# Block-diagonal level products, value products sorted by shape, and one projection moved, in a hybrid encoder layer

## The chip, the cores and the metric

One Trainium2 chip; the kernel runs on one of its cores. The metric is the device time of one execution in microseconds. Before the change three runs took 1318.72, 1318.90 and 1319.15 us; their median is 1318.9.

## The reference

One encoder layer over 1024 tokens of width 1024, in float32. One input projection feeds two groups of heads that run side by side; their outputs are normalised, gated, joined and projected; then come a layer norm, a SwiGLU feed-forward network, a second layer norm and a gated per-layer embedding (PLE). Cut to what the change touches:

```python
# HGRN2, 4 heads of 128, chunkwise:  S_t = diag(f_t) S_{t-1} + k_t (x) v_t,  k_t = 1 - f_t
scores  = einsum('bhtd,bhsd,bhtsd->bhts', q, k, decay)        # decay = exp(b_t - b_s) for s <= t
o       = einsum('bhts,bhsv->bhtv', scores, v) + einsum('bhtd,bhdv->bhtv', q * exp(b), state)
# mLSTM, 4 heads, q and k of 64, v of 128, stabilised, chunkwise
qk  = einsum('bhtd,bhsd->bhts', q, k) * w_intra
num = einsum('bhts,bhsv->bhtv', qk, v) + w_inter * einsum('bhtd,bhdv->bhtv', q, C)
den = sum(qk, -1) + w_inter * einsum('bhtd,bhd->bht', q, n)
# PLE, at the very end
x = x + sigmoid(x @ ple_w_gate + ple_b_gate) * (p @ ple_w_proj)
```

The decay in the HGRN2 scores differs for each of the 128 key channels, so `scores` isn't one matrix product of q and k.

## The kernel before, in words

**Precision.** The large products split each operand into a high and a low part (`split`, lines 75 to 77: a cast on ScalarE, a difference on VectorE) and sum three products in `mm3` (lines 79 to 83), each one record of 128x512 in the trace. The recurrences multiply plain float32, and each such product shows as two records.

**Stages.** `mixers` computes the input projection tile by tile and, between its matmuls, the two recurrences; `out_proj` the output projection and the first layer norm, with the first gate tiles of the network; `ffn_up` and `ffn_down` the network by a seven-product scheme on halves, with PLE at the end. A scheduler places the instructions: it keeps each engine's order near that of the program, but lets a later instruction go first where an earlier one isn't ready. TensorE, VectorE and ScalarE work off their queues in that order; loads are issued on SyncE's queue, stores on ScalarE's.

**The pumps.** Each recurrence is a Python generator with `yield` between its steps. `f_tile` (a tile of 128 projected channels, two halves of 512 tokens, 24 matmuls each) calls `pump` after half of the matmuls and at the end of a half, and `tok_group` and the PLE projection call it too; each call moves every live generator one step on. `finish` runs a generator to a mark or to its end at once. mLSTM's stream runs over all heads, `head(h)` computes f and q of one HGRN2 head and starts its stream, after it has run the head before to its tail. The last eight tiles (`gate_evac`) multiply the mixed values by their gates.

**HGRN2 levels** (`hgrn`, per head and half of the tokens, four chunks of 128). The triangle of scores A is built by levels L = 1, 2, 4, ... 64: at level L each block of 2L positions gets the products of its first half's keys with its second half's queries, and then q and k take in the decay of half a block (lines 567 and 568). For L = 1 (line 537) and L = 2 to 16 (line 556) the kernel multiplies all 128 keys by all 128 queries of a chunk (192 columns in the first product: the diagonal and level 1 together), and keeps the entries that a mask names, by a product with the unit matrix (line 538) and masked copies (lines 539 and 558). For L = 32 and 64 (line 549) it multiplies only the blocks, whose outputs start at partitions 0 and 64, or at 0. Score tiles rotate over three PSUM banks, of which the first product takes two for each half.

**mLSTM values** (`mlstm`, eight chunks). For each of two row halves q and two heads p of it, line 454 multiplies the scores E (128 rows) by the values, and from the second chunk on line 456 adds the state (64 rows) into the same place. The two kinds take turns. Line 465 updates the state with 64 stationary columns.

**PLE projection** (`ple_proj`, in `mixers`). p is multiplied by one half of the projection's columns between heads 1 and 2, by the other between heads 2 and 3; each time both weight tiles of p are loaded and split anew, results go by ScalarE (line 629) to memory, and `pump` is called four times.

**Memory.** Weight tiles of `mixers` and `out_proj` come from the pool wp (two raw, three split tiles). `ffn_up` opens its pools, with the split operands XS2, XS4 and XA22, where wp and out_proj's rows were; a tile there waits until the tile that lay there before is done with.

Of the kernel before, what the change touches and what calls it, by code (L numbers as in the profile page):

```python
# [9 lines left out]
F32 = mybir.dt.float32  # L10
F32R = mybir.dt.float32r
U8 = mybir.dt.uint8
# [6 lines left out]
P = 128  # L19
S = 1024  # L20
D = 1024
# [2 lines left out]
DFF = 2816  # L24
NF = DFF // P
HB = 512
EARLY = 4
NP = NF // 2
KORD = (4, 5, 6, 7, 0, 1, 2, 3)
LEVELS = (1, 2, 4, 8, 16, 32, 64)  # L30
ALPHA = 2.0 ** 0.25
LN_EPS = 1e-5
RMS_EPS = 1e-6
# [98 lines left out]
def mixers(g, es):  # L132
    a, act, dve, pool, pe, sp = g.a, g.act, g.dve, g.pool, g.pe, g.sp
    wtile, mm3, split, mtile = g.wtile, g.mm3, g.split, g.mtile
    kc = es.enter_context(g.tc.tile_pool(reuse_waits="tile", name="kc", bufs=1))
    mx = es.enter_context(g.tc.tile_pool(reuse_waits="tile", name="mx", bufs=2))
    ps = es.enter_context(g.tc.tile_pool(reuse_waits="tile", name="psA", bufs=1, space=PSUM))

    def bank(tag, shape, name):
        return ps.tile(shape, F32, tag=tag, bufs={"ft": 2, "hg": 3, "ml": 3}[tag], name=name)  # L140
# [23 lines left out]
    for k in range(KT):  # L164
        kk, q = divmod(k, 4)
# [6 lines left out]
        for b in range(2):  # L172
            raw = mtile("xraw")
            sp.dma_start(raw, a["xT"][:, k, b * HB:(b + 1) * HB])
            xraw.append(raw)
    for k in range(KT):
        kk, q = divmod(k, 4)
# [4 lines left out]
        for b in range(2):  # L182
            raw = xraw[2 * k + b]
# [22 lines left out]
    def stage(nm):  # L206
        return mx.tile([P, HB], F32, name="st", bufs=2)
# [14 lines left out]
    def pump():  # L222
        for st in list(streams):
            if next(st, "end") == "end":
                streams.remove(st)
# [99 lines left out]
    rcol = [kc.tile([64, P], F32, name=f"rcol{i}") for i in range(2)]  # L325
    for i in range(2):
        dve.memset(rcol[i], 0.0)
    lvl = kc.tile([P, 7, 256], U8)
    for l0, l1 in ((0, 4), (4, 7)):
        n = (l1 - l0) * 256  # L330
        raw = g.wp.tile([P, 1056], F32, name="wraw", bufs=2)
        rv = raw[:, :n].rearrange("p (l t) -> p l t", t=256)
        sp.dma_start(rv, a["lvl"][:, l0:l1])
        dve.tensor_copy(lvl[:, l0:l1], rv)
    ones_row = kc.tile([4, P], F32)
    dve.memset(ones_row, 1.0)
    Cst = kc.tile([P, 2, 129], F32)
    dve.memset(Cst, 0.0)
    mst = [kc.tile([4, 1], F32, name=f"mst{i}") for i in range(2)]
    dve.memset(mst[0], 0.0)  # L340
# [26 lines left out]
    def mlstm(c):  # L367
        i = c % 2
        qk = mx.tile([P, 4, P], F32, name="mqk")
        sp.dma_start(qk, g.mq_d[c])  # L370
        v = mx.tile([P, 4, 129], F32, name="mv")
        sp.dma_start(v[:, :, 0:P], g.mv_d[c].rearrange("p (h d) -> p h d", h=4))
        dve.memset(v[:, :, P:P + 1], 1.0)
        pg = bank("ml", [P, 2, P], "pg")
        pe.transpose(pg[0:4, 0], sm["ig"][:, c], ident)
        pe.transpose(pg[0:4, 1], sm["lf"][:, c], ident)
# [22 lines left out]
        ml = row("ml")  # L399
# [20 lines left out]
        pw = bank("ml", [P, 2, P], "pw")  # L420
        for p in range(2):
            pe.matmul(pw[:, p], sel[:, p], wrow[i], start=True, stop=True)
        qw = mx.tile([P, 2, P], F32, name="qw", bufs=1)
# [4 lines left out]
        pd = bank("ml", [P, 4, P], "pd")  # L428
# [18 lines left out]
        yield  # L447
        views = []
        den = mx.tile([P, 4], F32, name="den")
        for q in range(2):  # L450
            pr = slice(64 * q, 64 * q + 64)
            pn = bank("ml", [P, 2, 129], "pn")
            for p in range(2):
                pe.matmul(pn[:, p], E[:, 2 * p + q], v[:, 2 * p + q], start=True, stop=c == 0)
                if c:
                    pe.matmul(pn[:, p], qw[pr, p], Cst[pr, p], start=False, stop=True)
            dn = den[:, q::2]
            dve.tensor_max(dn, pn[:, :, P], cols[:, 32 + q:36:2])
            dve.scalar_tensor_tensor(dn, pn[:, :, P], -1.0, dn, op0=OP.mult, op1=OP.max)
            views.append((slice(q, 4, 2), pn[:, :, 0:P]))  # L460
        dve.reciprocal(den, den)
        if c < NC - 1:
            pst = bank("ml", [P, 2, 129], "pst")
            for h in range(4):
                pe.matmul(pst[64 * (h % 2):64 * (h % 2) + 64, h // 2], kws[:, h], v[:, h], start=True, stop=True)
            for p in range(2):
                dve.scalar_tensor_tensor(Cst[:, p], Cst[:, p], wold[:, p:p + 1], pst[:, p], op0=OP.mult, op1=OP.add)
# [50 lines left out]
    def hgrn(h, b, q, k, f):  # L518
# [3 lines left out]
        qq = q  # L522
# [5 lines left out]
        def odd(t):  # L528
            return t.rearrange("p c (b two) -> p c b two", two=2)[:, :, :, 1]

        A = mx.tile([P, 4, P], F32, name="A")
        dve.tensor_mul(q1, odd(q), odd(f))
        for c0 in (0, 2):
            cc = slice(c0, c0 + 2)
            pd = bank("hg", [P, 2, 192], "sc")
            for c in range(2):
                pe.matmul(pd[:, c], k[:, c0 + c], qq[:, c0 + c], start=True, stop=True)
            dve.tensor_mul(A[:, cc], pd[:, :, 0:P], ident[:, None, :].to_broadcast([P, 2, P]))
            dve.copy_predicated(odd(A[:, cc]), lvl[:, 0, 0:P].rearrange("p (c b) -> p c b", c=2), pd[:, :, P:192])
        dve.tensor_mul(even(q), even(q), even(f))  # L540
        tot = f.rearrange("p c t -> p (c t)")
        for li, L in enumerate(LEVELS):
            n = 2 * L
            if L >= 32:
                yield
                pd = bank("hg", [P, 4, P], "sc")
                for c in range(4):
                    for s in range(0, P, n):
                        pe.matmul(pd[s:s + L, c, 0:L], k[:, c, s:s + L], q[:, c, s + L:s + n], start=True, stop=True)
                for s in range(0, P, n):  # L550
                    act.copy(A[s:s + L, :, s + L:s + n], pd[s:s + L, :, 0:L])
            elif L > 1:
                yield
                pd = bank("hg", [P, 4, P], "sc")
                for c in range(4):
                    pe.matmul(pd[:, c], k[:, c], q[:, c], start=True, stop=True)
                vw = lambda t: t.rearrange("p h (b n) -> p (h b) n", n=n)[:, :, L:n]
                dve.copy_predicated(vw(A), lvl[:, li].rearrange("p (b l) -> p b l", l=L), vw(pd))
            nb = 256 // L
            tv = tot.rearrange("p (b two) -> p b two", two=2)  # L560
            t4 = tot.rearrange("p (c b two) -> p c b two", c=4, two=2)
            kv = k.rearrange("p h (b n) -> p (h b) n", n=n)[:, :, 0:L]
            if L == 1:
                dve.tensor_mul(odd(q), q1, t4[:, :, :, 0])
            else:
                qv = q.rearrange("p h (b n) -> p h b n", n=n)[:, :, :, L:n]
                dve.tensor_mul(qv, qv, t4[:, :, :, 0:1].to_broadcast([P, 4, nb // 4, L]))
            dve.tensor_mul(kv, kv, tv[:, :, 1:2].to_broadcast([P, nb, L]))
            nt = mx.tile([P, nb], F32, name=f"tot{L}", bufs=1 if L < 64 else 2)
            dve.tensor_mul(nt, tv[:, :, 0], tv[:, :, 1])  # L570
            tot = nt
# [43 lines left out]
        streams.append(head_streams[h])  # L615

    load_btok(520, 512)
    def ple_proj(s):
        pw = wtile(a["wpp"][s])
        for b in range(2):  # L620
            ph, pl = (t[:, :1024].rearrange("p (k t) -> p k t", k=2) for t in wtile(a["pT"][b]))
            for t in range(4):
                tt = slice(t * P, (t + 1) * P)
                pp = bank("ft", [P, 512], "pp")
                for k in range(2):
                    ks = slice(k * HB, (k + 1) * HB)
                    mm3(pp, (ph[:, k, tt], pl[:, k, tt]), tuple(w[:, ks] for w in pw), k == 0, k == 1)
                r = stage("ppo")
                act.copy(r, pp)
                act.dma_start(g.pp_d[4 * b + t, :, s * HB:(s + 1) * HB], r)  # L630
                if t % 2:
                    pump()

    tok_group("wt2", 0, g.hv_d, 0)
    head(0)
    tok_group("wt3", 256, g.hv_d, 256)
    head(1)
    ple_proj(0)
    head(2)
    ple_proj(1)  # L640
    head(3)

    for j in (4, 5, 6, 7, 0, 1, 2, 3):
# [10 lines left out]
def out_proj(g, es):  # L654
# [68 lines left out]
    transposed(1, y1)  # L723
    for f in range(2, EARLY):
        g.early[f] = g.ft.gate0(f)


def x_split(g, t, k0, b, raw=None):
# [385 lines left out]
def _shape_constants():  # L1114
    r = {}
    r["ident"] = np.eye(P, dtype=np.float32)
    s = np.arange(P)
    lvl = np.zeros((P, 7, 4, 64), np.float32)
    for li, L in enumerate(LEVELS):
        tsec = s[(s // L) % 2 == 1]  # L1120
        m = (s[:, None] // (2 * L) == tsec[None] // (2 * L)) & ((s[:, None] // L) % 2 == 0)
        lvl[:, li] = m[:, None, :]
    r["lvl"] = lvl.reshape(P, 7, 256)
    r["causal"] = np.where(s[:, None] <= s[None], 0.0, NEG).astype(np.float32)
    eye4 = np.zeros((P, 4), np.float32)
    eye4[:4] = np.eye(4)
    r["eye4"] = eye4
    sel = np.zeros((P, 4, P), np.float32)
    for p in range(2):
        for q in range(2):  # L1130
            for base in (0, 32):
                sel[base + 2 * p + q, p, 64 * q:64 * q + 64] = 1.0
    sel[0:4, 2] = 1.0
    sel[32:36, 2] = 1.0
    r["sel"] = sel
    ind = np.zeros((P, 4, P), np.float32)
    for h in range(4):
        ind[64 + h, h] = 1.0
        ind[96 + h, h] = 1.0
    r["ind"] = ind  # L1140
    return r
# [19 lines left out]
```

## Time and profile before

The profiled execution took 1320.13 us, its span is 1318.3 us; what lies around the span is 1.8 us.

| | |
|---|---|
| profiled execution, its span | 1320.13 us, 1318.3 us |
| granted TensorE clock, mean | 0.995 |
| DMA, mean over the span | 147 GB/s |
| share of the chain that ended last, by TensorE | 87% |
| the same, by VectorE | 8% |

How to read the lines. A group line has the source line (that of a helper where a helper records the instruction), the engine, the operation, the tiles written and read, TensorE's active rows and columns (128*32 is 128 rows and 32 columns), shape, count, busy time in us and mean length in ns, and then the idle time just before and what ended it. A timeline line has start, length, engine, line, operation, tiles, shape and count. TensorE overlaps its matmuls and the ends are modelled, so lengths add up to more than the time they take; the distance between starts is the better measure. A line of windows has the stretch, its length, the busy time and count of each engine, the granted clock, the share of the DMA engines and their rate.

### The profile page before, as it was taken

What the parts mean: (1) busy time and instruction counts of PE and PEld (TensorE: products, weight loads), DVE (VectorE), ACT (ScalarE), POOL (GpSimd) and SP (SyncE); (2) the same over time, 40 slices, a digit from 0 to 9 for tenths busy, and PEclk for the clock granted to TensorE, in tenths of its full rate; (3) what the DMA queues carried; (4) which work ended last, traced back from release to release, by engine and by line L of the source; (5) the groups of instructions that cost most, each with busy time, mean ns of one, the idle gap of its engine ahead of it and who ended that gap; (6) DMA issues with size and microseconds to landing.
All of it is one profiled execution on the core that took longest, in us unless ns stands there. A gap on an engine that the chain in (4) does not pass through costs nothing.

```text
span 1318.3 us, 17022 instructions
## 1 busy us (share of the span) xinstructions
PE 1296.9 (98%) x6616; PEld 1078.8 (82%) x6616; DVE 906.1 (69%) x1577; ACT 471.7 (36%) x649; POOL 28.0 (2%) x36
## 2 busy tenths in 40 slices
PE   9999999999999999997999999999999999999998
PEld 8899888888888878775888888888888788888787
DVE  7646776767663275478887777877776974559974
ACT  4422414454523251443243333333333333333241
POOL 0000000000000000000000000000000000000000
PEclk9999999999999999998999999999999999999999
DMA  7354112323111175323564345445428976554442
GB/s 246 112 161 140 57 44 78 122 71 129 33 33 33 48 289 176 125 96 107 189 197 154 132 172 184 142 154 184 152 102 300 334 254 192 198 201 150 152 148 76
DMA packets 87185, 193.35 MB, mean 147 GB/s; under 512 B 8384, under 2 KB 26560, under 8 KB 81344
## 3 DMA queue, kind: packets, MB, share of 16 engines
q1 hardware_dynamic: 52832, 133.26, 30.7%
q10 hardware_dynamic: 34272, 59.00, 12.1%
q8 instruction: 52, 0.85, 0.3%
q14 instruction: 29, 0.24, 0.1%
HBM read 141.63 MB, written 50.59 MB: 146 GB/s over the span
## 4 chain that ended last, share of the span: by engine, by line
PE 87%; DVE 8%; issue 1%; DMA 1%; ACT 1%; POOL 1%; SPq 0%; POOLq 0%; DVEq 0%; ACTq 0%
PE ft L82 7%; PE ft L83 7%; PE ft L81 7%; PE y L81 3%; PE y L83 3%; PE x L82 3%; PE y L82 3%; PE x L83 3%; PE x L81 3%; PE z L83 3%; PE z L82 3%; PE z L81 3%; PE pg L81 2%; PE pg L83 2%; PE dnb L82 2%; PE pg L82 2%
## 5 line engine op out<-in xcount | busy, mean ns | idle before, releaser
L81 PE MATMUL ft<-xh,whl 128*128 128x512 f32 x320 | 128.5, 402 | 0.0
L77 DVE TENSOR_TENSOR whl<-hw,whl 128x2048 fp32r<-128x2048 f32 (+1 forms) x42 | 88.4, 2106 | 56.6 <-ACT whl L76 56.6
L83 PE MATMUL ft<-xh,whl 128*128 128x512 f32 x320 | 127.2, 398 | 0.0
L82 PE MATMUL ft<-xl,whl 128*128 128x512 f32 x320 | 126.9, 396 | 0.0
L76 ACT CAST whl<-hw 128x2048 fp32r<-128x2048 f32 (+1 forms) x42 | 74.2, 1772 | 119.7 <-PE dna L83 43.5
L77 DVE TENSOR_TENSOR whl<-wraw,whl 128x1024 fp32r<-128x1024 f32 x64 | 77.7, 1217 | 39.9 <-ACT whl L76 39.8
L76 ACT CAST whl<-wraw 128x1024 fp32r<-128x1024 f32 x64 | 66.7, 1051 | 94.7 <-PE wo L83 37.0
L76 ACT CAST hl<-gu 128x1024 fp32r<-128x1024 f32 (+1 forms) x48 | 46.8, 981 | 77.6 <-PE x L83 56.4
L81 PEld LDWEIGHTS ft<-xh,whl 128*128 128x128 f32 x320 | 61.1, 191 | 12.7 <-issue 0.2
L82 PE MATMUL x<-XS,hl 128*128 128x512 f32 x176 | 69.4, 394 | 1.3 <-DVE XS L77 1.3
L83 PEld LDWEIGHTS ft<-xh,whl 128*128 128x128 f32 x320 | 60.1, 188 | 12.7
L82 PEld LDWEIGHTS ft<-xl,whl 128*128 128x128 f32 x320 | 60.2, 188 | 11.9
L82 PE MATMUL dna<-whl 128*128 128x512 f32 x176 | 68.6, 390 | 1.2 <-DVE whl L77 1.2
L81 PE MATMUL z<-XA,hl 128*128 128x512 f32 x176 | 68.8, 392 | 0.9 <-ACT p L756 0.7
L81 PE MATMUL x<-XS,hl 128*128 128x512 f32 x176 | 69.2, 393 | 0.0
L83 PE MATMUL x<-XS,hl 128*128 128x512 f32 x176 | 69.0, 392 | 0.0
L83 PE MATMUL z<-XA,hl 128*128 128x512 f32 x176 | 68.5, 390 | 0.2 <-DVE hl L77 0.2
L82 PE MATMUL z<-XA,hl 128*128 128x512 f32 x176 | 68.5, 389 | 0.0
L81 PE MATMUL dna<-whl 128*128 128x512 f32 x176 | 68.5, 389 | 0.0
L83 PE MATMUL dna<-whl 128*128 128x512 f32 x176 | 68.5, 389 | 0.0
L76 ACT CAST hl<-tt 128x1024 fp32r<-128x1024 f32 (+1 forms) x44 | 36.8, 836 | 63.6 <-PE w L83 27.1
L77 DVE TENSOR_TENSOR hl<-gu,hl 128x1024 fp32r<-128x1024 f32 (+1 forms) x48 | 54.1, 1131 | 6.1 <-ACT hl L76 6.1
(297 smaller groups left out, 3204.9 us busy)
## 6 DMA issues: line engine op xcount, KB each, us to landing
gu<-in_wgu SPq DMA_DIRECT2D x26, 1024.0 KB, 5.1
hw<-h_d SPq DMA_DIRECT2D x35, 512.0 KB, 4.0
wdp<-in_wd SPq DMA_DIRECT2D x11, 1024.0 KB, 5.0
h_d<-hs ACTq DMA_DIRECT2D x44, 256.0 KB, 3.6
wraw<-in_wf SPq DMA_DIRECT2D x20, 512.0 KB, 3.7
hw<-w_d SPq DMA_DIRECT2D x20, 512.0 KB, 5.0
w_d<-wdp ACTq DMA_DIRECT2D x33, 256.0 KB, 2.8
wraw<-in_wo SPq DMA_DIRECT2D x16, 512.0 KB, 3.7
```

The lines of the kernel that those rows point to most:

```text
L76: g.act.copy(hi, raw)
L77: g.dve.tensor_sub(lo, raw, hi.bitcast(F32))
L81: g.pe.matmul(acc, lh, rh, start=first, stop=False, skip_group_check=more)
L82: g.pe.matmul(acc, lh, rl, start=False, stop=False, skip_group_check=more)
L83: g.pe.matmul(acc, ll, rh, start=False, stop=last, skip_group_check=more)
```

## The change

Three edits, and what they need.

1. HGRN2: for the diagonal and the levels 1 to 16 only blocks of 32 positions on the diagonal are multiplied, each with an output at its own partitions 0, 32, 64 or 96, into a tile D of 128 partitions x 4 chunks x 32 columns. The diagonal and level 1 are two products for each block, of 32 and of 16 columns, and take one bank a half instead of two. Masks and unit matrix shrink to 32 columns. After level 16, ScalarE copies D's blocks into A, of which there are now two fixed copies, cleared once by GpSimd.
2. mLSTM: the four E products of a chunk come first and the four state products behind them, with a bank for each row half open at the same time.
3. PLE: the projection stands at the end of `out_proj`, behind the last early gate tile; both halves of its columns are done together, so that each weight tile of p is loaded and split once; results leave through an own pair of tiles. Its eight calls of `pump` in `mixers` are gone.

```diff
+VW = P + 1
+BK = 32
+NB = P // BK
+NLV = 5
...
-    lvl = kc.tile([P, 7, 256], U8)
...
+    lvl = kc.tile([P, NLV, 64], U8)
...
+    eye = g.const("eye32", kc)
+    Ab = [kc.tile([P, 4, P], F32, name=f"A{i}") for i in range(2)]
+    for t in Ab:
+        pool.memset(t, 0.0)
...
+        pns = [bank("ml", [P, 2, VW], "pn") for _ in range(2)]
         for q in range(2):
-            pr = slice(64 * q, 64 * q + 64)
-            pn = bank("ml", [P, 2, 129], "pn")
             for p in range(2):
-                pe.matmul(pn[:, p], E[:, 2 * p + q], v[:, 2 * p + q], start=True, stop=c == 0)
-                if c:
-                    pe.matmul(pn[:, p], qw[pr, p], Cst[pr, p], start=False, stop=True)
+                pe.matmul(pns[q][:, p], E[:, 2 * p + q], v[:, 2 * p + q], start=p == 0, stop=c == 0,
+                          skip_group_check=True)
+        if c:
+            for q in range(2):
+                pr = slice(64 * q, 64 * q + 64)
+                for p in range(2):
+                    pe.matmul(pns[q][:, p], qw[pr, p], Cst[pr, p], start=False, stop=True, skip_group_check=True)
...
-        A = mx.tile([P, 4, P], F32, name="A")
+        A = Ab[b]
+        D = mx.tile([P, 4, BK], F32, name="D")
         dve.tensor_mul(q1, odd(q), odd(f))
-        for c0 in (0, 2):
-            cc = slice(c0, c0 + 2)
-            pd = bank("hg", [P, 2, 192], "sc")
-            for c in range(2):
-                pe.matmul(pd[:, c], k[:, c0 + c], qq[:, c0 + c], start=True, stop=True)
-            dve.tensor_mul(A[:, cc], pd[:, :, 0:P], ident[:, None, :].to_broadcast([P, 2, P]))
-            dve.copy_predicated(odd(A[:, cc]), lvl[:, 0, 0:P].rearrange("p (c b) -> p c b", c=2), pd[:, :, P:192])
+
+        def blocks(dst, rhs, n):
+            for c in range(4):
+                for j in range(NB):
+                    s = slice(j * BK, (j + 1) * BK)
+                    pe.matmul(dst[s, c], k[:, c, s], rhs[:, c, j * n:(j + 1) * n], start=True, stop=True)
+
+        pd = bank("hg", [P, 4, BK + BK // 2], "sc")
+        blocks(pd[:, :, 0:BK], q, BK)
+        blocks(pd[:, :, BK:], q1, BK // 2)
+        dve.tensor_mul(D, pd[:, :, 0:BK], eye[:, None, :].to_broadcast([P, 4, BK]))
+        dve.copy_predicated(odd(D), lvl[:, 0].rearrange("p (c b) -> p c b", c=4), pd[:, :, BK:])
...
             elif L > 1:
                 yield
-                pd = bank("hg", [P, 4, P], "sc")
-                for c in range(4):
-                    pe.matmul(pd[:, c], k[:, c], q[:, c], start=True, stop=True)
+                pd = bank("hg", [P, 4, BK], "sc")
+                blocks(pd, q, BK)
...
-                dve.copy_predicated(vw(A), lvl[:, li].rearrange("p (b l) -> p b l", l=L), vw(pd))
+                dve.copy_predicated(vw(D), lvl[:, li].rearrange("p (b l) -> p b l", l=L), vw(pd))
+                if n == BK:
+                    for j in range(NB):
+                        s = slice(j * BK, (j + 1) * BK)
+                        act.copy(A[s, :, s], D[s])
...
     head(1)
-    ple_proj(0)
     head(2)
-    ple_proj(1)
     head(3)
...
     for f in range(2, EARLY):
         g.early[f] = g.ft.gate0(f)
+    pw = [wtile(a["wpp"][s]) for s in range(2)]
+    for b in range(2):
+        ph, pl = (t[:, :1024].rearrange("p (k t) -> p k t", k=2) for t in wtile(a["pT"][b]))
+        for t in range(4):
+            tt = slice(t * P, (t + 1) * P)
+            for s in range(2):
+                pp = acc_bank("pp")
+                for k in range(2):
+                    ks = slice(k * HB, (k + 1) * HB)
+                    mm3(pp, (ph[:, k, tt], pl[:, k, tt]), tuple(w[:, ks] for w in pw[s]), k == 0, k == 1)
+                r = g.wp.tile([P, HB], F32, name="ppo", bufs=2)
+                act.copy(r, pp)
+                act.dma_start(g.pp_d[4 * b + t, :, s * HB:(s + 1) * HB], r)
```

More of the change, by code (lines that the diff above doesn't have):

```diff
@@ L327, in mixers @@
         dve.memset(rcol[i], 0.0)
-    lvl = kc.tile([P, 7, 256], U8)
[L329 to L334, printed above, removed]
+    lvl = kc.tile([P, NLV, 64], U8)
+    lvr = g.wp.tile([P, 1056], F32, name="wraw", bufs=2)
+    lvv = lvr[:, :NLV * 64].rearrange("p (l t) -> p l t", t=64)
+    sp.dma_start(lvv, a["lvl"])
+    dve.tensor_copy(lvl, lvv)
+    eye = g.const("eye32", kc)
+    Ab = [kc.tile([P, 4, P], F32, name=f"A{i}") for i in range(2)]
+    for t in Ab:
+        pool.memset(t, 0.0)
     ones_row = kc.tile([4, P], F32)
     dve.memset(ones_row, 1.0)
-    Cst = kc.tile([P, 2, 129], F32)
+    Cst = kc.tile([P, 2, VW], F32)
     dve.memset(Cst, 0.0)
@@ L370, in mlstm @@
         sp.dma_start(qk, g.mq_d[c])
-        v = mx.tile([P, 4, 129], F32, name="mv")
+        v = mx.tile([P, 4, VW], F32, name="mv")
         sp.dma_start(v[:, :, 0:P], g.mv_d[c].rearrange("p (h d) -> p h d", h=4))
-        dve.memset(v[:, :, P:P + 1], 1.0)
+        dve.memset(v[:, :, P:VW], 1.0)
         pg = bank("ml", [P, 2, P], "pg")
@@ L449, in mlstm @@
         den = mx.tile([P, 4], F32, name="den")
+        pns = [bank("ml", [P, 2, VW], "pn") for _ in range(2)]
         for q in range(2):
-            pr = slice(64 * q, 64 * q + 64)
-            pn = bank("ml", [P, 2, 129], "pn")
             for p in range(2):
-                pe.matmul(pn[:, p], E[:, 2 * p + q], v[:, 2 * p + q], start=True, stop=c == 0)
-                if c:
-                    pe.matmul(pn[:, p], qw[pr, p], Cst[pr, p], start=False, stop=True)
+                pe.matmul(pns[q][:, p], E[:, 2 * p + q], v[:, 2 * p + q], start=p == 0, stop=c == 0,
[5 more added lines that the diff above has]
+                    pe.matmul(pns[q][:, p], qw[pr, p], Cst[pr, p], start=False, stop=True, skip_group_check=True)
+        for q in range(2):
+            pn = pns[q]
             dn = den[:, q::2]
@@ L462, in mlstm @@
         if c < NC - 1:
-            pst = bank("ml", [P, 2, 129], "pst")
+            pst = bank("ml", [P, 2, VW], "pst")
             for h in range(4):
@@ L617, in mixers @@
     load_btok(520, 512)
[L618 to L632, printed above, removed]
     tok_group("wt2", 0, g.hv_d, 0)
@@ L1117, in _shape_constants @@
     s = np.arange(P)
[L1118 to L1121, printed above, removed]
+    sb = s % BK
+    lvl = np.zeros((P, NLV, 4, BK // 2), np.float32)
+    for li, L in enumerate(LEVELS[:NLV]):
+        tsec = s[:BK][(s[:BK] // L) % 2 == 1]
+        m = (sb[:, None] // (2 * L) == tsec[None] // (2 * L)) & ((sb[:, None] // L) % 2 == 0)
         lvl[:, li] = m[:, None, :]
-    r["lvl"] = lvl.reshape(P, 7, 256)
+    r["lvl"] = lvl.reshape(P, NLV, 64)
+    r["eye32"] = (sb[:, None] == s[None, :BK]).astype(np.float32)
     r["causal"] = np.where(s[:, None] <= s[None], 0.0, NEG).astype(np.float32)
```

## The prediction

> **What bounds the kernel now.** I read the page first, then the windows, then the timeline around each edited place. The page has the span and the engines:
>
> ```profile
> span 1318.3 us, 17022 instructions
> PE 1296.9 (98%) x6616; PEld 1078.8 (82%) x6616; DVE 906.1 (69%) x1577; ACT 471.7 (36%) x649; POOL 28.0 (2%) x36
> ```
>
> TensorE is the bound, so an edit is worth what it takes off TensorE's queue, or out of the few places where TensorE waits. The profiled execution took 1320.1 us, 1.2 us above the median of the runs; I sum against 1320.1 and subtract 1.2 at the end. The windows show where TensorE is not full (columns: length; busy time of PE, PEld, DVE, ACT, POOL; granted clock; DMA share; GB/s):
>
> ```profile
> 231.00:400.00 169.00, 167.17 (x1072) 137.96 (x1071) 121.82 (x356) 73.51 (x129) 9.16 (x8) 1.00 0.24 75
> 575.00:595.00 20.00, 16.94 (x83) 13.24 (x81) 15.19 (x25) 15.18 (x26) 0.00 (x0) 1.00 0.22 79
> 595.00:625.00 30.00, 24.21 (x83) 17.58 (x82) 25.20 (x40) 10.54 (x19) 0.00 (x0) 0.83 0.30 102
> 625.00:700.00 75.00, 74.82 (x329) 61.33 (x328) 66.19 (x95) 24.95 (x34) 0.00 (x0) 1.00 0.55 186
> ```
>
> In the mixers (231 to 400 holds heads 1 to 3 and both pieces of the PLE projection) TensorE waits for almost nothing and VectorE is at 72%. Between 575 and 625, from out_proj into ffn_up, TensorE idles 9 us and runs at a mean clock of 0.83.
>
> **HGRN2 level products.** Two groups of the view by line and shape (count | busy us, mean ns | idle before), then clean stretches of both kinds of product from the timeline (start, length, line, shape, count); the left-out lines are projection matmuls:
>
> ```profile
> L556 PE MATMUL sc<-q,k 128*128 128x128 f32 x256 | 32.2, 277 | 1.6 <-DVE k L568 1.6
> L558 DVE COPY_PREDICATED A<-lvl,sc 128x256 f32<-128x256 uint8 x32 | 16.1, 504 | 6.8 <-PE sc L556 6.6
> ```
> ```profile
> 363.79 0.40 PE L83 MATMUL ft<-xh,whl 128*128 128x512 f32 x1
> 364.03 1.46 PE L537 MATMUL sc<-q,k 128*128 128x192 f32 x8
> ...
> 365.93 0.89 PE L537 MATMUL sc<-q,k 128*128 128x192 f32 x4
> ...
> 366.89 0.86 PE L537 MATMUL sc<-q,k 128*128 128x192 f32 x4
> ...
> 367.82 0.40 PE L82 MATMUL ft<-xl,whl 128*128 128x512 f32 x1
> ...
> 369.21 0.40 PE L82 MATMUL ft<-xl,whl 128*128 128x512 f32 x1
> 369.44 0.40 PE L83 MATMUL ft<-xh,whl 128*128 128x512 f32 x1
> 369.68 1.95 PE L556 MATMUL sc<-q,k 128*128 128x128 f32 x16
> ...
> 371.69 0.39 PE L82 MATMUL ft<-xl,whl 128*128 128x512 f32 x1
> ```
>
> Durations overlap, so I price a stretch by what it pushes the projection matmuls apart: those start 0.23 us after each other when undisturbed (369.21 to 369.44). A float32 product shows as two records. Sixteen L556 records, from the matmul before to the second one after, cost 371.69 - 369.44 - 2 x 0.23 = 1.79 us, 0.112 each; 256 cost 28.7 us. Head 3's sixteen L537 records lie between 363.79 and 367.82, and five projection intervals with them: 4.03 - 5 x 0.23 = 2.88 us; four heads, 11.5 us. Removed: **40.2 us**.
>
> Added, per head and half: 64 records for the diagonal (32 products) and 32 for each of the levels 2, 4, 8, 16; times eight, 1536 records with 32 stationary columns, on four column groups (outputs at partitions 0, 32, 64, 96). The nearest rows are level 32's, of the same shape on two column groups:
>
> ```profile
> 265.72 0.40 PE L83 MATMUL ft<-xh,whl 128*128 128x512 f32 x1
> 266.05 0.45 PE L549 MATMUL sc<-q,k 128*32 128x32 f32 x16
> ...
> 266.75 0.40 PE L82 MATMUL ft<-xl,whl 128*128 128x512 f32 x1
> ...
> 388.69 0.40 PE L83 MATMUL ft<-xh,whl 128*128 128x512 f32 x1
> 389.02 0.70 PE L549 MATMUL sc<-q,k 128*32 128x32 f32 x32
> ...
> 389.99 0.39 PE L82 MATMUL ft<-xl,whl 128*128 128x512 f32 x1
> ...
> 392.31 0.40 PE L83 MATMUL ft<-xh,whl 128*128 128x512 f32 x1
> 392.64 1.15 PE L549 MATMUL sc<-q,k 128*64 128x64 f32 x16
> ...
> 394.05 0.39 PE L82 MATMUL ft<-xl,whl 128*128 128x512 f32 x1
> ```
>
> Thirty-two records cost 0.84 us and sixteen 0.57: 17 ns a record and 0.30 us for entering and leaving the narrow shape. The third stretch, level 64's, has one column group and streams 64 columns where level 32 streams 32; it costs (1.74 - 0.46 - 0.30) / 16 = 61 ns a record. Half of that, 31 ns, is a 32-column record on one group, so two groups at 17 ns overlap almost wholly. Four could halve 17 to 8.5 ns; or something shared, such as dispatch, could hold it at 17. I take 11, nearer the halving, because two groups show hardly a loss. With 22 stretches (five per head, a few split): 1536 x 0.011 + 22 x 0.30 = 23.5 us. Gain **16.7 us**, ends 7.5 (17 ns) and 20.5 (8.5 ns). VectorE also loses work: the masked copies (L558) take in a quarter of the elements. ScalarE gains 32 small copies of D into A; at 44% (73.51 of 169) it has room: nothing. The cleared A tiles, the smaller lvl and the eye32 load come early, on engines that wait there: nothing.
>
> **mLSTM value products.** A chunk with both kinds, the first chunk (no state) and a row-halved stretch in two banks:
>
> ```profile
> 138.46 0.38 PE L454 MATMUL pn<-mv,E 128*128 128x129 f32 x2
> 138.77 0.49 PE L456 MATMUL pn<-Cst,qw 64*128 64x129 f32 x2
> ...
> 141.69 0.66 PE L465 MATMUL pst<-mv,kws 128*64 128x129 f32 x8
> ```
> ```profile
> 114.71 1.05 PE L454 MATMUL pn<-mv,E 128*128 128x129 f32 x8
> 115.69 0.66 PE L465 MATMUL pst<-mv,kws 128*64 128x129 f32 x8
> ```
> ```profile
> 233.03 0.72 PE L438 MATMUL pq<-mqk 64*128 64x128 f32 x8
> 233.68 0.44 PE L443 MATMUL pk<-c_ident,mqk 128*128 128x128 f32 x2
> ```
>
> Alternating shapes, the sixteen records take 141.69 - 138.46 = 3.23 us. Sorted, the eight E records take 0.98 (115.69 - 114.71, the shape change behind them included) and the eight state records the 0.65 of L438, which has the same row halves in two banks. 3.23 - 1.63 = 1.60 us for each of seven chunks: **11.2 us**. If the halves did not overlap, eight records of 0.11 and a change of shape (1.1 us in all) leave 1.15 a chunk, 8.1 us. The second bank is taken earlier, but from the same rotation of three; the denominators on VectorE wait for the whole group, which now ends sooner. No cost.
>
> **PLE projection moved.** Its TensorE work goes along:
>
> ```profile
> L81 PE MATMUL pp<-whl 128*128 128x512 f32 x32 | 13.5, 420 | 0.0
> L77 DVE TENSOR_TENSOR whl<-wraw,whl 128x1024 fp32r<-128x1024 f32 x64 | 77.7, 1217 | 39.9 <-ACT whl L76 39.8
> L76 ACT CAST whl<-wraw 128x1024 fp32r<-128x1024 f32 x64 | 66.7, 1051 | 94.7 <-PE wo L83 37.0
> ```
>
> Three lines of 32 at 0.23 us are 22 us, taken from the mixers and put back behind gate0. Two of six weight tiles are no longer loaded and split (SyncE, ScalarE 2.1, VectorE 2.4 us; none bounds). What matters is the cover. At the new place TensorE waits now:
>
> ```profile
> 592.01 0.39 PE L83 MATMUL z<-XA,hl 128*128 128x512 f32 x1
> 594.54 0.50 PE L81 MATMUL y<-XS,hl 128*128 128x512 f32 x1 [2.14 <-ACT hl L76]
> ...
> 612.78 0.40 PE L83 MATMUL y<-XA,hl 128*128 128x512 f32 x1
> 617.00 0.79 PE L81 MATMUL y<-XS,hl 128*128 128x512 f32 x1 [3.82 <-ACT hl L76]
> ```
>
> Gaps of 2.3 and 4.0 us, and low clock after them (0.17 of 30 us, at most 5.1). VectorE, 25.2 of 30 us busy, is what is late: it builds ffn_up's split operands. 22 us of TensorE work that asks VectorE for four splits (4.9 us) lets it get ahead, so the first gap goes. The second shrinks only: XS2, XS4 and XA22 lie where the wp pool was, whose weight tiles the projection holds to its end, so their twelve splits follow it. I give 8 us back, less 2.3 for the second pT tile (1.05 + 1.22), whose buffer the first half frees: **6 us**. Ends: -3 (no gap goes, the pT wait is paid) and 13 (all gaps and low clock). ScalarE's queue gets sixteen evacuations and DMA issues ahead of ffn_up's casts, SyncE's four loads ahead of later weights; ScalarE is idle there for half of the time (25.7 of 50 us busy) and the DMA share is 0.22 to 0.30.
>
> In the mixers the cover is lost: eight of the pump calls that advance the recurrences go with the projection, so heads 1 and 2 run their last steps, and mLSTM its last chunk, in one go, with only projection matmuls that are ready to fill in. Heads 1 to 3 shrink to about 169 - 22 - 13 - 6 = 128 us (the projection, three quarters of 16.7, four chunks at 1.6), VectorE to some 106 (121.8 less 6 x 1.2 for splits, and about 8 of the 24 x 0.50 of L558): 83%, under the 88% (66.19 of 75) that TensorE bears without idling at 625 to 700. I charge **-5 us**, ends 0 and -12.
>
> **Sum.** 16.7 + 11.2 + 6 - 5 = 28.9. 1320.1 - 28.9 - 1.2 = **1290 us**.
>
> **Rivals.**
> *Dispatch holds narrow matmuls at the pace of two groups.* For: no stretch quoted has narrow records closer than 17 ns. Against: two groups already overlap almost without loss. 17 instead of 11 ns costs 9.2 us: 1299.
> The Trainium skill, "TensorE: Matmul & The Clock Gate", section "Wait — 56ns, not 53.3ns?", speaks against the change: start-to-start never drops below about 25 ns however few columns stream. By it the blocks would cost 1536 x 0.025 + 6.6 = 45 us, 4.8 more than they replace, and the time would be an estimated 1311 (11.2 + 6 - 5 - 4.8 off). The trace disagrees: 17 ns.
> *The cover is missed.* For: VectorE's rise from 72 to 83%, and the pumps. Against: the 625 to 700 row. Stalls of 12 us and nothing filled at the new place (-3): 16 us less gain, 1306.
> *Long narrow runs starve (slower).* The longest narrow run in the trace has 32 records; the new diagonals have 128 for both halves, the levels 64. If records past the 32nd fell to the one-group pace of 61 ns, 4 x 96 + 16 x 32 = 896 records would cost 50 ns more each, 45 us: 1335. It decides from 32 ns more (28.9 / 896), 43 ns a record. Against: the run of 32 is as fast per record as the run of 16.
> *The move does nothing* (gaps covered anyway elsewhere): 6 us, 1296; inside the range and the forecast's chance.
>
> **How the numbers follow.** Forecast 0.53, two-group pace 0.23, missed cover 0.16, starving 0.05, and 0.03 for small mishaps that cancel the gain. A measurement tells about 0.2%, 2.6 us. Faster 0.92, same 0.03, slower 0.05. All good ends together give 1274 (20.5 + 11.2 + 13 off), all bad ones 1318 (7.5 + 8.1 - 3 - 12); leaving a tenth at each side, 1276 to 1308.
>
> **What would show it.** TensorE records rise to 6616 - 64 - 256 + 1536 = 7832. A level run of 64 narrow records spans under 1 us, a diagonal of 128 under 1.8 (over 2.2: two-group pace; over 4: starving). L454's eight records stand together and the next pst starts 1.6 us after them. The first y starts within 0.5 us of the last pp, the second y within 2 us of the product before, with no low clock. In the mixers no wait over 2 us before a ft matmul. I am wrong if narrow runs are slow, or if TensorE's idle time in the mixers grows by over 12 us.

## The result: 1296.3 us, and the profile after

The changed kernel takes 1296.32 us (median of four runs, 1295.19 to 1297.78), the kernel before beside it 1319.03 us: a ratio of 0.9829, interval 0.9812 to 0.9846. It is faster by 22.7 us, inside the range, and 6 us short of the forecast of 28.9. The profiled execution took 1297.29 us. The page of after, its span and engines:

```profile
span 1295.5 us, 19441 instructions
PE 1268.9 (98%) x7832; PEld 1050.5 (81%) x7832; DVE 884.3 (68%) x1558; ACT 483.8 (37%) x683; POOL 28.5 (2%) x38
```

The record count is the forecast one. TensorE is still the bound; its busy time fell by 28.0 us (1296.9 - 1268.9), the span by 22.8. So 5 us of what was taken off TensorE came back as time in which it waits.

Where, is read from the starts of the first out_proj (wo) and first ffn_up (y) products. The view by tile of before, then of after (count; shortest, median and longest ns; first to last start):

```profile
L81 PE MATMUL wo<-whl,mixh x128: 389/389/499, 470.3 to 563.4; 128*128 128x512 f32 x128
L81 PE MATMUL y<-XS,hl x88: 389/389/793, 594.5 to 989.9; 128*128 128x512 f32 x88
```
```profile
L85 PE MATMUL wo<-whl,mixh x128: 388/390/497, 427.9 to 521.0; 128*128 128x512 f32 x128
L85 PE MATMUL y<-XS,hl x88: 388/389/501, 573.3 to 967.1; 128*128 128x512 f32 x88
```

Up to wo the kernel gained 42.4 us; up to y only 21.2, because the projection's 22.1 us now lie between. The rest gains 1.6 more. The same starts were read from every trace below, counted from the first product of the input projection (which starts between 4.5 and 5.6 us). Two traces of the kernel after, this one and that of its second run, agree to 0.1 us in the first two columns, and differ by 1.3 and 0.7 in the others; between kernels, y to ffn_down scatters from 405.5 to 409.7, though none but e10 differs in what it does there:

| kernel | mixers (to wo) | wo to y | y to ffn_down | ffn_down to the end |
|---|---|---|---|---|
| before | 465.6 | 124.2 | 409.7 | 314.1 |
| after | 422.2 | 145.4 | 408.0 | 314.2 |
| e1: products only, PLE back | 438.6 | 124.2 | 407.6 | 313.5 |
| e2: blocks only | 450.9 | 124.0 | 409.1 | 313.8 |
| e3: sorted only | 455.1 | 124.2 | 407.9 | 314.3 |
| e4: PLE only | 448.1 | 147.3 | 406.9 | 314.2 |
| e5: after, more pumps | 417.6 | 145.4 | 408.0 | 313.7 |
| e6: after, PLE ahead of the gates | 422.9 | 140.4 | 407.4 | 313.2 |
| e7: after, other loop order | 436.4 | 147.0 | 405.5 | 313.5 |
| e8: after, blocks twice | 449.0 | 145.4 | 408.2 | 313.7 |
| e9: e5 and e6 | 417.9 | 140.2 | 406.4 | 313.7 |
| e10: e9, sums later | 417.4 | 140.2 | 428.8 | 314.0 |

**The new products.** Two clean narrow stretches in the timeline of after (start, length, line, shape, count). Both are first products, the diagonal with level 1: half of their records stream 32 columns, half 16.

```profile
153.41 0.28 PE L87 MATMUL ft<-whl,xl 128*128 128x256 f32 x1
153.62 1.33 PE L550 MATMUL sc<-q,k 128*32 128x32 f32 x128
154.88 0.38 PE L85 MATMUL ft<-whl,xh 128*128 128x256 f32 x1
155.10 0.28 PE L86 MATMUL ft<-whl,xh 128*128 128x256 f32 x1
155.22 0.28 PE L87 MATMUL ft<-whl,xl 128*128 128x256 f32 x1
...
318.55 0.40 PE L87 MATMUL ft<-xh,whl 128*128 128x512 f32 x1
318.87 0.75 PE L550 MATMUL sc<-q,k 128*32 128x32 f32 x64
319.55 0.50 PE L85 MATMUL ft<-xh,whl 128*128 128x512 f32 x1
319.89 0.40 PE L86 MATMUL ft<-xl,whl 128*128 128x512 f32 x1
```

Priced as in the prediction: the diagonals of both halves, 128 records, push the 256-column products, 0.12 us apart when undisturbed (155.10 to 155.22), apart by 155.10 - 153.41 - 2 x 0.12 = 1.45 us. The diagonal of one half, 64 records, costs 319.89 - 318.55 - 2 x 0.23 = 0.88. The difference gives 0.57 / 64 = 9 ns a record and leaves 0.31 us for entering and leaving the narrow shape. The width hardly counts: a level of 64 records that all stream 32 columns spans 0.76 us (at 163.49), this diagonal 0.75.

The mLSTM chunk of the same place as the quoted one of before:

```profile
139.38 1.05 PE L459 MATMUL pn<-mv,E 128*128 128x129 f32 x8
140.37 0.72 PE L465 MATMUL pn<-Cst,qw 64*128 64x129 f32 x8
141.02 0.66 PE L476 MATMUL pst<-mv,kws 128*64 128x129 f32 x8
```

Sixteen records took 3.23 us in turns; sorted they take 1.64 (139.38 to 141.02).

**The windows** of after, for heads 1 to 3 and for what follows the projection (length; PE, PEld, DVE, ACT, POOL; clock; DMA share; GB/s):

```profile
231.00:360.00 129.00, 122.34 (x1731) 95.78 (x1731) 95.61 (x323) 66.88 (x131) 8.62 (x8) 1.00 0.13 40
573.00:610.00 37.00, 31.83 (x123) 24.26 (x121) 26.74 (x42) 14.89 (x27) 0.00 (x0) 0.91 0.31 102
```

TensorE lacked 1.8 of 169 us in these heads; now it lacks 6.7 of 129, while VectorE is at only 74% (95.61 of 129). And the weak place between out_proj and ffn_up is still there: 5.2 idle us in 37 and a mean clock of 0.91. The timeline of after shows its waits (in brackets: idle before, and what ended it; hl are the split weights, XS and XA the split operands):

```profile
539.00 0.39 PE L87 MATMUL z<-XA,hl 128*128 128x512 f32 x1
541.42 0.50 PE L85 MATMUL z<-XA,hl 128*128 128x512 f32 x1 [2.03 <-ACT p L772]
...
560.60 0.39 PE L87 MATMUL pp<-whl 128*128 128x512 f32 x1
562.12 0.50 PE L85 MATMUL pp<-whl 128*128 128x512 f32 x1 [1.13 <-ACT whl L80]
...
573.08 0.39 PE L87 MATMUL pp<-whl 128*128 128x512 f32 x1
573.31 0.40 PE L85 MATMUL y<-XS,hl 128*128 128x512 f32 x1
...
578.54 0.39 PE L87 MATMUL x<-XS,hl 128*128 128x512 f32 x1
580.16 0.49 PE L85 MATMUL w<-XS,hl 128*128 128x512 f32 x1 [1.23 <-ACT XS L80]
582.43 0.80 PE L86 MATMUL w<-XS,hl 128*128 128x512 f32 x1 [1.78 <-DVE XS L81]
...
593.81 0.40 PE L87 MATMUL y<-XA,hl 128*128 128x512 f32 x1
595.91 0.50 PE L85 MATMUL y<-XS,hl 128*128 128x512 f32 x1 [1.71 <-ACT hl L80]
```

The first y follows the last pp at once: the 2.3 us gap of before is gone. But 2.2 us are lost between two gate products at 539 (541.42 - 539.00 - 0.23), 1.3 at the second weight tile of p, 3.4 at the two w products (1.39 and 2.04), 1.9 at the second y. The low clock isn't behind the second y here: it follows the w waits. From 583 to 587 us the window shows 0.50, and the w products start 0.43 us apart instead of 0.23; from 589 on it shows 1.00, also behind the second y. In the trace of the second run of this kernel the waits are the same, but the clock is back at 1.00 by 585, and the mean of the same 37 us is 0.95. VectorE and ScalarE in the same stretch:

```profile
579.04 0.69 DVE L876 TENSOR_TENSOR p<-x,p 128x512 f32<-128x512 f32 x1 [15.71 <-PE x L87]
```
```profile
576.73 0.59 ACT L740 COPY ppo<-pp 128x512 f32<-128x512 f32 x1
...
578.97 0.62 ACT L80 CAST hl<-tt 128x512 fp32r<-128x512 f32 x1 [1.64 <-PE x L87]
579.49 4.25 ACT L80 CAST XS<-x1T 128x512 fp32r<-128x512 f32 x8
```

VectorE, which was to get ahead during the projection, did nothing for 15.7 us, from 563.3 to 579.0; the last 5.7 of them lie behind the projection's last product. Most of the casts that it needed (XS) ran on ScalarE only after the last copy of the projection, and behind a cast that waits for TensorE.

### The profile page after: what moved, and what is told of

Read it like the earlier page. It is cut to its first block, busy times and chain, and to the rows that moved or that the text cites. A ratio compares the mean times of both kernels' runs of the same rounds, so it can differ in the third digit from the quotient of the medians.

```text
span 1295.5 us, 19441 instructions
## 1 busy us (share of the span) xinstructions
PE 1268.9 (98%) x7832; PEld 1050.5 (81%) x7832; DVE 884.3 (68%) x1558; ACT 483.8 (37%) x683; POOL 28.5 (2%) x38
## 4 chain that ended last, share of the span: by engine, by line
PE 84%; DVE 8%; ACT 2%; DMA 2%; issue 1%; POOL 1%; SPq 0%; POOLq 0%; ACTq 0%; DVEq 0%
PE ft L85 7%; PE ft L86 7%; PE ft L87 7%; PE x L85 3%; PE x L86 3%; PE x L87 3%; PE y L85 3%; PE y L86 3%; PE y L87 3%; PE z L85 3%; PE z L86 3%; PE z L87 3%; PE pg L85 2%; PE pg L87 2%; PE pg L86 2%; PE wo L85 2%
## 5 line engine op out<-in xcount | busy, mean ns | idle before, releaser
L876 DVE TENSOR_TENSOR p<-x,p 128x512 f32<-128x512 f32 x22 | 15.2, 691 | 71.1 <-PE x L87 68.6
```

The costliest lines, as they stand in the source:

```text
L876: dve.tensor_sub(p7, x, p7)
```

## The experiments

All results, each with the kernel before on the same chip:

| kernel | median us | lowest to highest, runs | ratio to before | interval |
|---|---|---|---|---|
| e1_ple_back | 1293.43 | 1290.18 to 1295.44, 5 | 0.9807 | 0.9793 to 0.9820 |
| e2_blocks_only | 1302.12 | 1300.16 to 1304.75, 4 | 0.9868 | 0.9854 to 0.9882 |
| e3_sorted_only | 1309.52 | 1308.28 to 1310.94, 5 | 0.9923 | 0.9911 to 0.9936 |
| e4_ple_only | 1322.35 | 1319.36 to 1324.51, 11 | 1.0016 | 1.0007 to 1.0025 |
| e5_more_pumps | 1291.77 | 1290.86 to 1294.42, 4 | 0.9797 | 0.9783 to 0.9810 |
| e6_ple_before_gates | 1290.57 | 1289.51 to 1291.72, 4 | 0.9784 | 0.9771 to 0.9798 |
| e7_group_major | 1308.72 | 1308.42 to 1312.49, 5 | 0.9929 | 0.9916 to 0.9941 |
| e8_blocks_twice | 1325.28 | 1322.96 to 1327.30, 4 | 1.0052 | 1.0037 to 1.0068 |
| e9_both | 1284.79 | 1284.48 to 1286.47, 5 | 0.9744 | 0.9731 to 0.9757 |
| e10_sums_later | 1308.87 | 1307.00 to 1309.06, 5 | 0.9919 | 0.9907 to 0.9932 |
| after_again | 1295.75 | 1294.76 to 1297.07, 4 | 0.9823 | 0.9810 to 0.9837 |

### The parts alone: e1 to e4

The first question was which edit lacks the 6 us. e1 is the changed kernel with the projection back in the mixers:

```diff
     head(1)
+    ple_proj(0)
     head(2)
+    ple_proj(1)
     head(3)
...
     for f in range(2, EARLY):
         g.early[f] = g.ft.gate0(f)
-    pw = [wtile(a["wpp"][s]) for s in range(2)]
-    for b in range(2):
...
```

> The kernel after, with the PLE projection and its eight pump calls back in the mixers: edits 1 and 2 alone. By the two traces edits 1 and 2 take 28.3 us off TensorE (17.1 for the blocks: 1536 records at 9 ns and 30 stretches at 0.31 us against 40.2; 11.2 for the sorted products), the mixers shrink by 7 us less than that, and the projection costs 19.6 instead of 22 us at its new place. Theory A, the 7 us are the cover and the pumps that went with the projection: they come back here, 1319.0 - 28.3 = 1291 us, 5 us faster than the kernel after, and the ft waits of 0.6 to 2.2 us between 230 and 340 us are gone. Theory B, the 7 us come from TensorE catching up with VectorE's chain whatever fills it: they stay, 1298 us, 1 to 2 us slower than the kernel after.

e2 is e1 with the mLSTM products in turns again, so of the change it holds the blocks alone:

```diff
-        pns = [bank("ml", [P, 2, VW], "pn") for _ in range(2)]
         for q in range(2):
+            pr = slice(64 * q, 64 * q + 64)
+            pn = bank("ml", [P, 2, VW], "pn")
             for p in range(2):
...
+                if c:
+                    pe.matmul(pn[:, p], qw[pr, p], Cst[pr, p], start=False, stop=True)
```

> The kernel before with edit 1 alone (block products of the HGRN2 levels). TensorE loses 17.1 us. Theory A (stalls come from the moved projection): 1302 us. Theory B (TensorE catches up with VectorE's chain): 3 to 6 us of the 17 lost to waits for VectorE's q and k updates, 1305 to 1308 us.

e3 and e4 are the kernel before with one edit each, the sorted products and the moved projection:

```diff
+        pns = [bank("ml", [P, 2, 129], "pn") for _ in range(2)]
...
+        if c:
+            for q in range(2):
...
```

> The kernel before with edit 2 alone (mLSTM value products sorted by row count). Both theories: seven chunks at 1.60 us, 11.2 us off TensorE; A says all of it shows, 1307.8 us; B lets up to 2 us of it go to waits, 1308 to 1310 us.

```diff
     head(1)
-    ple_proj(0)
     head(2)
-    ple_proj(1)
     head(3)
...
         g.early[f] = g.ft.gate0(f)
+    pw = [wtile(a["wpp"][s]) for s in range(2)]
+    for b in range(2):
...
```

> The kernel before with edit 3 alone (PLE projection behind out_proj). Gain of 2.4 us at the new place in both theories. Theory A, the lost cover and pumps cost 7 us: 1319.0 - 2.4 + 7 = 1323.6 us, slower than before. Theory B, the mixers lose nothing while TensorE still has the wide level products to do: 1316.6 us.

The kernel before took 1319.81 us beside these four. The blocks alone gain 17.7 us (forecast 16.7), the sorting 10.3 (11.2), both together 26.4 (27.9). The move alone loses 2.5 us by the medians (ratio 1.0016, 1.0007 to 1.0025), where it was to gain 1 (6 - 5). Beside the other two edits it loses about the same: the ratio rises from 0.9807 (e1) to 0.9829, 2.9 us. (The intervals of these two ratios overlap a little; that of e4 alone excludes no change.) So the missing 6 us lie mostly with the move, as theory A had it; the product edits lack 1.5. A's numbers came out for e2 (1302) and within 1.3 us for e4 (1323.6); e1 is 2.4 us above A's 1291, and e3's 1309.5 lies in B's range of 1308 to 1310.

The stages say where it loses. In e1 the mixers shrink by 27.0 us of the 28.3 that TensorE is spared (40.2 - 23.1 for the blocks, as worked out further on, and 11.2), so the products lose 1.3 there. With the projection gone, too, they shrink by 43.4 of 50.4: the move's own share of the loss is 5.7 us, in e4 4.6. At the new place, from wo to y, the 22.1 us come back as 21.2 (e4: 23.1).

### Why the mixers lose: e5

Two things went with the projection: work for TensorE that was always ready, and eight calls of `pump`. e5 gives back pumps alone: the f and q tiles of heads 2 and 3 pump twice inside a half instead of once, eight calls more.

```diff
-    def f_tile(i, evac, w=None):
+    def f_tile(i, evac, w=None, at=(3,)):
...
-                if k == 3:
+                if k in at:
                     pump()
...
-        f_tile(h, evac)
+        f_tile(h, evac, at=(2, 5) if h >= 2 else (3,))
...
-        f_tile(4 + h, evac)
+        f_tile(4 + h, evac, at=(2, 5) if h >= 2 else (3,))
```

> The kernel after, with three pump calls instead of two in each half of the f and q tiles of heads 2 and 3: the eight calls that went with the projection are given back, without its TensorE work. Theory A1, the mixers' 5.7 to 7 us are lost because the recurrences have too few steps before finish: they come back, ratio to before 0.979 (1292 us), and the 2 us wait for ScalarE's k at 307 us in the kernel after is gone. Theory A2, what is lost is TensorE work to lay between steps: no gain or up to 3 us more, ratio 0.983 to 0.985.

The mixers fell from 422.2 to 417.6 us: 4.6 of the 7.0 that they lacked. TensorE's waits from 150 to 360 us, the longest sums of after and then of e5 (us in total, times, longest):

```profile
PE ft L85 <- ACT k L509: 2.0, 1, 2.0
PE ft L85 <- ACT q L521: 1.1, 2, 0.6
```
```profile
PE sc L566 <- DVE k L588: 1.8, 2, 1.3
PE sc L550 <- DVE D L574: 1.7, 3, 0.8
```

After's waits of projection matmuls (ft) for the evacuations of the f and q tiles (L509 makes k of the f tile, L521 makes q) are no longer there. In after, the evacuation behind the wait of 2.0 us stood in ScalarE's queue behind a step of mLSTM (306.62) and an ACT_TABLE_LOAD of 1.28 us (307.02). The move also raised the number of such loads: 30 in before and e1, 34 in after and e4, 33 in e5. So the eight calls, without any TensorE work, bring back most of what the mixers lost. What no run shows is what eight more calls would gain where the projection still stands in the mixers; part of the 4.6 us could be had there as well.

### Where the projection stands: e6

Theory P was that the projection's hold on the wp memory makes XS late, and that ahead of the early gate tiles 2 and 3 it would be done before XS is wanted.

```diff
-    for f in range(2, EARLY):
-        g.early[f] = g.ft.gate0(f)
     pw = [wtile(a["wpp"][s]) for s in range(2)]
     for b in range(2):
...
                 act.dma_start(g.pp_d[4 * b + t, :, s * HB:(s + 1) * HB], r)
+    for f in range(2, EARLY):
+        g.early[f] = g.ft.gate0(f)
```

> The kernel after, with the PLE projection ahead of the last two early gate tiles instead of behind them. Theory P, the projection does not help at its place since it holds the wp pool's memory until ffn_up's first products, so VectorE idles from 557 to 579 us with XS2, XS4 and XA22 not yet allowed: now the gate tiles' 11 us lie between, the waits of w at 578 to 582 us (3.8 us) and of the second y (1.9 us) shrink to under 2 in all and the low clock goes, 4 to 7 us less than the kernel after, ratio 0.978 to 0.980. Rival, VectorE's total work there sets the time and only moves: within 1.5 us of the kernel after, ratio 0.982 to 0.984.

From wo to y it takes 140.4 us instead of 145.4, and the time falls to 1290.57. The w waits and the wait at the gate are gone: from 520 to 620 us only two sums of TensorE's waits are left, of which the first grew. The waits of e6, then its window behind the last pp and the second y in its timeline:

```profile
PE y L85 <- ACT hl L80: 3.6, 1, 3.6
PE pp L85 <- ACT whl L80: 1.1, 1, 1.1
```
```profile
573.00:610.00 37.00, 33.45 (x135) 26.62 (x134) 29.93 (x46) 12.84 (x22) 0.00 (x0) 0.91 0.37 123
```
```profile
584.21 0.39 PE L87 MATMUL y<-XA,hl 128*128 128x512 f32 x1
588.15 0.80 PE L85 MATMUL y<-XS,hl 128*128 128x512 f32 x1 [3.55 <-ACT hl L80]
```

P was right on the gain and half right on the place: the second y now waits 3.7 us (588.15 - 584.21 - 0.23), nearly the 4.0 of before, and a low clock follows this wait (mean 0.91). e6 frees the wp memory earlier and puts the projection's copies elsewhere in ScalarE's queue; which of the two held the XS casts back, no run separates.

### The order of the narrow products: e7

The blocks are issued so that successive products write partitions 0, 32, 64, 96 in turn. e7 exchanges the loops: four products (eight records) in a row on the same column group.

```diff
-            for c in range(4):
-                for j in range(NB):
+            for j in range(NB):
+                for c in range(4):
```

> The kernel after, with the two loops of the block products exchanged: the four chunks of one column group come one after the other, so eight records on the same group in a row. Theory G, narrow records are cheap (9 ns) because four column groups run side by side: in this order only neighbouring runs overlap, up to 31 ns a record (the one-group pace worked out from level 64), at most 1536 x 22 = 34 us more, and a stretch of 64 spans 1.5 to 2 us instead of 0.76. Rival, a 32-column record costs 9 ns whatever its group: no change.

Two stretches of e7's timeline:

```profile
327.95 0.40 PE L87 MATMUL ft<-xh,whl 128*128 128x512 f32 x1
328.28 1.50 PE L550 MATMUL sc<-q,k 128*32 128x32 f32 x64
329.71 0.50 PE L85 MATMUL ft<-xh,whl 128*128 128x512 f32 x1
330.04 0.40 PE L86 MATMUL ft<-xl,whl 128*128 128x512 f32 x1
```

These 64 records, again one half's diagonal, cost 330.04 - 327.95 - 0.46 = 1.63 us against after's 0.88: 21 ns a record instead of 9 ((1.63 - 0.31) / 64). So the overlap of the four groups makes the pace, and it needs them in turn. It costs less than the 31 ns estimated for one group alone; that the last record of a group and the first of the next still overlap would explain it, but isn't shown. The mixers grew by 14.2 us, not by 1536 x 12 ns = 18: TensorE's waits from 150 to 380 us fell to two, of 2.0 and 0.5 us. A slower TensorE seems to have hidden part of what it had waited for.

### Twice as many: e8

e8 issues each block product twice, the second time with the same result into the same place. It tests whether long narrow runs slow down.

```diff
-            for c in range(4):
+            for c in list(range(4)) * 2:
```

> The kernel after, with every block product issued twice (the same result is written again): 1536 more narrow records in the same stretches. At 9 ns each and with TensorE as the bound, 13.8 us more, about 1310 us. If stretches longer than those of the kernel after starve (theory of the slower rival: 61 ns past some length), 30 us or more. If TensorE's waits for VectorE take up part of it, 7 to 12 us.

In the timeline of e8, the rest of a doubled diagonal behind a wait, and a doubled level that none interrupts:

```profile
235.39 0.82 PE L550 MATMUL sc<-q,k 128*32 128x32 f32 x60 [3.01 <-issue]
...
362.87 0.40 PE L87 MATMUL ft<-xh,whl 128*128 128x512 f32 x1
363.20 1.37 PE L550 MATMUL sc<-q,k 128*32 128x32 f32 x128
364.50 0.50 PE L85 MATMUL ft<-xh,whl 128*128 128x512 f32 x1
364.84 0.40 PE L86 MATMUL ft<-xl,whl 128*128 128x512 f32 x1
```

A level of 128 records costs 1.51 us here (364.84 - 362.87 - 0.46): (1.51 - 0.31) / 128 = 9 ns. No slowing. Yet the time rose by 29 us and the mixers by 26.8, where 1536 x 9 ns make 14. That is near the 30 us or more of the starving theory, but not by its mechanism, since a record still costs 9 ns. Most of the other 13 us is waiting: from 231 to 385 us TensorE is idle for 16.3 us (after: 6.7 in its 129), and the mean clock there is 0.98. Before level products 5.6 us of waits, the quoted 3.01 among them, have no releaser in the profile. What they wait for stays open.

### Both mends: e9, and the last wait: e10

e9 puts e5 and e6 together; its diff is theirs.

> The kernel after with both repairs: twelve instead of eight steps for each of heads 2 and 3, and the PLE projection ahead of the last two early gate tiles. They sit in different stages (mixers 4.6 us, out_proj into ffn_up 5 us by their traces). If the two losses are independent they add: 1296 - 4.6 - 5.6 = 1286 us, ratio 0.975. If one only moves the other's wait, 1290 us, ratio 0.978.

It takes 1284.79 us, 0.9744 [0.9731, 0.9757] of the kernel before, the fastest of all: the mixers 417.9, wo to y 140.2, each as in its own experiment. The two losses are independent. TensorE is busy for 1263.9 us of a span of 1282.8, 99%.

The second y's wait is left. In e10 the sums of ffn_down's weights, VectorE work of each even tile, are done in the odd tiles: theory V held that they make VectorE late there, ahead of the second y.

```diff
             put(S3, i, s3)
-            wd_sums(i)
             continue
+        wd_sums(i)
```

> The kernel e9_both, with the sums of the down weights (four VectorE additions, 2.5 us, for two feed-forward tiles) made in the odd tiles instead of the even ones, so not in the first. Theory V, the wait of 3.7 us ahead of the second y and the low clock behind it come from VectorE's load in the first tile: 2 to 5 us less than e9_both, ratio 0.971 to 0.974. Rival, the wait is for something else in that chain (the masked-out buffers hl and tt): no change against e9_both.

V fell: the second y still waits 3.55 us. And the time rose to 1308.87, since a new wait stands ahead of ffn_down:

```profile
PE dna L85 <- ACT whl L80: 21.5, 1, 21.5
PE y L85 <- ACT hl L80: 4.8, 2, 3.6
```

ScalarE's cast of the first ffn_down weights had waited 18.20 us for their load there. The last sums now fall into the last tile; that their weight tile holds the memory of that load is argued, not tested. As for the second y, e9's timeline of ScalarE shows what stands ahead of the casts that it needs (hl):

```profile
580.07 0.63 ACT L896 ACTIVATE c<-c 128x512 f32<-128x512 f32 x1 [6.08 <-DVE c L895]
580.72 1.14 ACT L80 CAST hl<-gu 128x512 fp32r<-128x512 f32 x2
```

They come in the queue behind an activation (c) of the tile before, which waits for that tile's last product. ScalarE is idle for 6.08 us, then starts casting only as TensorE has run dry. The kernel after has the other order, the casts first:

```profile
594.30 0.62 ACT L80 CAST hl<-gu 128x512 fp32r<-128x512 f32 x1 [2.75 <-PE y L87]
594.82 1.04 ACT L80 CAST hl<-tt 128x1024 fp32r<-128x1024 f32 x1
595.77 0.63 ACT L896 ACTIVATE c<-c 128x512 f32<-128x512 f32 x1
```

There the second y waits 1.71 us. All thirteen traces agree: where the activation comes first (before, e1, e2, e3, e6, e9, e10) the wait is 3.55 to 3.83 us, where the casts come first (after in both runs, e4, e5, e7, e8) it is 1.71. The order came about by the scheduler and goes with the place of the projection; no run changes it alone.

### The kernel after once more

> The kernel after itself, on the same chip as the two repairs. Both theories: ratio 0.983 within its interval; it gives the distance of the repairs from it on one chip.

1295.75 us, 0.9823 [0.9810, 0.9837]: the first result again.

## Why the prediction was right, and where it missed

- **Blocks, 23.5 us added, gain 16.7.** Right: measured 17.7 alone. That it is so near is in part luck, since two misses cancel in the working: a record takes 9 ns, not 11, and there are 30 stretches, not 22, since the two halves of a level often run apart (the trace of after has 32 runs, two of them the rest of a run cut short): 1536 x 9 ns + 30 x 0.31 = 23.1. The choice "nearer the halving" was right, and could go further: four groups overlap wholly.
- **Dispatch holds 17 ns; long runs starve.** Both fell: 9 ns in runs of 64 and of 128, in e8 too. The Trainium skill, "TensorE: Matmul & The Clock Gate", section "Wait — 56ns, not 53.3ns?", gives about 25 ns as the least start-to-start; the 9 ns measured here do not agree, and the measurement decides. The same page, section "Part 3: Packing small matmuls — row/col tiling", says that small products on different tiles of the array run at the same time, and that an output's start partition picks its column tile; e7 agrees, 21 ns with four products in a row on one group and 9 ns with groups in turn.
- **Sorted mLSTM, 11.2.** Right: 3.23 to 1.64 us a chunk, seven times 1.59 is 11.1; alone 10.3.
- **Mixers' lost cover, -5.** Right in size: 7.0 us of the 50.4 (28.3 + 22.1) are missing, 5.7 by the move and 1.3 by the products. The reason was half right. I bounded it by VectorE's load, which I put at 83% and 106 us; it is 74% and 95.6, and VectorE is not what is late. The pumps are, for most of it (e5), which I had named beside it.
- **Move, +6 at the new place.** This is the step that failed: "22 us of TensorE work that asks VectorE for four splits (4.9 us) lets it get ahead, so the first gap goes. ... I give 8 us back, less 2.3 for the second pT tile". The first gap did go, 2.3 us; there the reason held, for in before the cast ahead of the first y had waited 2.06 us for VectorE. The second shrank from 4.0 to 1.9, but not by VectorE's work: ScalarE's casts came ahead of an activation there (see e10). And VectorE didn't get ahead, it stood idle for 15.7 us, because most of the casts that feed it came from ScalarE after the projection. I had written that XS2 lies where the wp pool was and that its splits follow the projection; I charged that to the second gap and not to the products that read XS first. Waits of 2.2 us at the gate and 3.4 at w, and the 1.3 forecast as 2.3, took back nearly all. From wo to y the move gains 0.9 us in after and loses 1.0 in e4; behind y the 1.7 us that after gains are near the 1.3 by which its own two traces differ. So between -1 and 2.6 us where I gave 6.
- **The move does nothing (1296).** This rival's number is what came out, though by another road: e4 shows that the move, with its loss in the mixers, costs 2.5 us.
- **The cover is missed (1306).** Less than that: the mixers lost 7.0, not 12, and the new place gained a little.
- **Marks.** Records 7832; runs of 64 in 0.76 us and of 128 in 1.33; E products together and pst 1.64 us behind; y 0.23 us behind pp: all as written. Missed: the second y came 2.10 us after the product before (595.91 - 593.81), and there was a low clock, though behind the w products and not behind the second y. The longest wait before a ft matmul is 2.0 us, on the line.

The sum again with what was measured: products 26.4 instead of 27.9, the move about -3 instead of +1 (-2.5 in e4, -2.9 by the ratios of e1 and after; 22.7 - 26.4, from two chips, gives -3.7). The prediction was right by the products, not by the move.

## What to carry to other kernels

Where only blocks on a diagonal are wanted, issue them as narrow products that rotate over the column groups, and put products of one shape together: the shape change and the order cost more than the columns. A step that is moved takes its calls to other generators along, and holds its memory and fills ScalarE's queue at the new place; ask which tiles lie over that memory, and behind what in the queue their first instruction then stands. Put back in other steps what the moved step did on the side, and try the step a few tiles earlier: these two small mends together (e9) were worth 11 us more.

## What the hardware showed

- A float32 record with 32 stationary and 16 or 32 streamed columns costs 9 ns with four column groups in turn, 21 with four products (eight records) in a row on one group; with two groups and 32 streamed columns it cost 17 in before. The granted clock was 0.99 to 1.00; runs of up to 128 change nothing.
- Entering and leaving the narrow shape costs 0.31 us together; sixteen records of two row counts cost 1.6 us more when they take turns.
- Equal waits are followed by low clocks of unequal length. With a wait of 3.55 us ahead of the second y the mean over 573 to 610 us was 0.91 in e6 and 0.95 in e9; two runs of the kernel after, both with waits of 1.23 and 1.78 us at the w products, had 0.91 and 0.95. The wait of 1.71 us ahead of after's second y was followed by a clock of 1.00.
- How long TensorE stood ahead of the second y went with the order of two steps in ScalarE's queue: 1.71 us with the casts ahead of the waiting activation, 3.55 to 3.83 behind it, in thirteen traces.
